# Two groups of eight mixer tiles by seven products, the other six plainly at the stage's end; the residual on VectorE straight from PSUM

## The chip, the cores and the metric

The kernel runs on one core of one Trainium2 chip. A core has five engines with a queue of instructions each: TensorE (PE in the profile, its weight loads PEld), VectorE (DVE), ScalarE (ACT), GpSimd (POOL) and SyncE (SP), which here only issues DMAs. Data lie in SBUF (128 partitions); matmuls write PSUM, eight banks of 128 x 512 floats. The metric is the device time of one execution in microseconds (us).

## The reference

A trunk of four layers on x (512 tokens, 1024 features, float32). Each layer is a token mixer (convolution, neighbourhood attention, retention, convolution) and then a gated channel mixer, each behind an RMS norm and added to x. Cut to what matters here:

```python
D_MODEL, SEQ, DEPTH = 1024, 512, 4
FFN_DIM = 2816                      # 22 tiles of 128

def conv_ffn(h, w_up, dw_w, dw_b, w_down):
    u = dwconv(h @ w_up, dw_w, dw_b)        # 5632 columns, 3 taps over tokens
    val, gate = jnp.split(u, 2, axis=-1)
    return (jax.nn.gelu(gate) * val) @ w_down

for i in range(DEPTH):
    h = rmsnorm(x, norm1_g[i])
    x = x + token_mixer(i, h)
    h = rmsnorm(x, norm2_g[i])
    x = x + conv_ffn(h, ffn_w_up[i], ffn_dw_w[i], ffn_dw_b[i], ffn_w_down[i])
```

## The kernel before

**Layout and precision.** x stays in SBUF, features on partitions, as eight tiles `x[0]` to `x[7]` of 128 x 512. A float32 product is made of three: each operand is split into a high part (cast to fp32r) and a low part (the rest), and `mm3` (L168 to L171) issues high x high, high x low, low x high. Weights come by DMA on SP into the two buffers `wr`; `split_w` (L161 to L166) casts the high part on ACT (L164) and subtracts on DVE (L165), into three buffers each of `wh` and `wl`. `prep` (L226, called `after` where a stage ends) makes the next stage's input from a tile of x: high part on ACT (L236), low part on DVE (L239), and `squares` (L250), a square on ACT whose sum into `sqacc` is made on POOL by default (L257).

**The mixer stage, `ffn` (L283).** It runs once for each layer. The 44 column tiles of the up-projection (`up`, L288, 24 wide matmuls each) are made in pairs, value and gate. `mid(j)` (L323) applies the three taps, gelu and product to pair j and gives tile j of the hidden layer, 22 in all; TensorE works on `ups_of` (L511) for the next pair meanwhile.

**Seven products.** The down-projection takes two hidden tiles (a pair of tiles, as two halves of the inner dimension), two outputs (`x[2i]`, `x[2i+1]`) and two halves of the tokens, and multiplies the 2 x 2 blocks by seven products instead of eight (Strassen-Winograd). `mid` builds the seven sums of the hidden side in F and splits them into Hh and Hl (four slots of each, `SLOT_H`); `weights` (L392) builds those of the weights: two are loaded, one is accumulated by a POOL DMA (L402), others are summed on DVE. `prod` (L420) issues one product over the pairs of a part, three narrow matmuls (256 columns) a pair. `down(q)` (L444) runs part q for the four output pairs i: products 1, 6, 0, 4, 5 in the banks xb and v, then, one output pair later, `finish` (products 2 and 3 and the add L451 into `x[2i+1]`).

**The residual of a part.** `x[2i+1]` is carried by the tile s12: ACT copies (L467, L470) and a POOL DMA that accumulates x onto it (L474); L451 then adds it to the bank v. `x[2i]` goes likewise: ACT copies the negated bank xc to u2, a POOL DMA accumulates x (L487), and DVE subtracts v (L488). In the last output pair of the last part (`direct`) DVE does it without a DMA.

**Order in a stage.** Tiles 0 and 1 (`REST`) are kept out of the products. `PARTS` groups the other ten pairs as 3, 3 and 4. The first two parts start inside the stage, after pairs 8 and 14 of the up-projections, and `filler` puts the next pair of up-projections between the last output pair's products and its `finish`. At the end of the stage stand `remainder` (tiles 0 and 1 plainly, ACT copy, POOL DMA accumulating into x) and the part of four pairs, after each of whose outputs `after` prepares the input of the next stage.

Of the kernel before, what the change touches and what calls it, by code (L numbers as in the profile page):

```python
# [70 lines left out]
PARTS = ((0, 3), (3, 6), (6, 10))  # L71
PART_COL = (0, 1536, 3072)
REST = 2
SLOT_H = 4
NT_FFN = 7
# [5 lines left out]
def tile_trunk(  # L81
# [168 lines left out]
    def squares(k, src, perm=False, eng=nc.gpsimd, wait=False):  # L250
        sq = t512() if k else sqacc
        nc.scalar.activation(sq.rearrange("p (c r) -> p r c", r=8) if perm else sq, src, AF.Square)
        if k == 0 and wait:
            state["wait"] = nc.gpsimd.tensor_copy(sm(1), xlo[KD - 1][:, :1].bitcast(F32))
        if k:
            with tc.issue_after(state["wait"].ins) if wait else ExitStack():
                eng.tensor_tensor(sqacc, sq, sqacc, ADD)  # L257
# [25 lines left out]
    def ffn(l, after):  # L283
        with ExitStack() as st:
            stage_pools(st, NT_FFN, 8, 0)
            hp = st.enter_context(tc.tile_pool(name=nm("ffn"), bufs=1, reuse_waits=RW))
            last = len(PARTS) - 1
# [35 lines left out]
            def mid(j, pv, pg):  # L323
# [17 lines left out]
                if j < REST:  # L341
                    nc.vector.tensor_tensor(acc[0], acc[0], acc[1], MUL)
                    hi = hp.tile([P, T], F32R, tag=f"rh{j}", name=nm("hh"))
                    lo = hp.tile([P, T], F32R, tag=f"rl{j}", name=nm("hl"))
                    split(acc[0], hi, lo)
                    rest[j] = (hi, lo)
                    return
                p = (j - REST) // 2
# [43 lines left out]
            def weights(i, q, gate=None):  # L392
# [14 lines left out]
                r2 = hp.tile([P, T], F32, tag="w2", name=nm("w2"))  # L407
                nc.vector.tensor_tensor(r2[:, :n], r13[:, n:2 * n], r1[:, :n], ADD)
                h2 = hp.tile([P, T], F32R, tag="h2", name=nm("h2"))
                l2 = hp.tile([P, T], F32R, tag="l2", name=nm("l2"))  # L410
                split(r2[:, :n], h2[:, :n], l2[:, :n])
                nc.vector.tensor_tensor(sg[:, :n], r2[:, :n], sg[:, n:2 * n], ADD)
# [15 lines left out]
            def rest_weights(c, gate):  # L428
                with tc.issue_after(gate.ins):
                    raw = load_raw(f_rest[l, :, c], D)  # L430
                return split_w(raw, D, nc.vector)

            def remainder(ws):
                for c, (wh, wl) in enumerate(ws):
                    for o in range(4):
                        ps = bank(psa)
                        for k in range(REST):
                            s = slice((o * REST + k) * P, (o * REST + k + 1) * P)
                            mm3(ps, wh[:, s], wl[:, s], *rest[k], k == 0, k == REST - 1)
# [4 lines left out]
            def down(q, first, pieces=iter(()), filler=None):  # L444
                final = q == last
                p0, p1 = PARTS[q]

                def finish(i, w, v, s12):
# [3 lines left out]
                    if final:  # L452
                        after(2 * i + 1)

                prev = None
                for i in range(4):
                    w = weights(i, q) if i else first
                    direct = final and i == 3
# [19 lines left out]
                    u2h, vh, xh2 = (t.rearrange("p (h t) -> p h t", h=2) for t in (u2, v, x[2 * i]))  # L478
                    if direct:
                        nc.scalar.activation(u2[:, :256], xc, AF.Copy, scale=-1.0)  # L480
                        nc.vector.tensor_tensor(x[2 * i], x[2 * i], v, SUB)
                        nc.vector.tensor_tensor(
                            xh2, xh2, u2h[:, :1, :].broadcast_to([P, 2, 256]), ADD)
                    else:
                        nc.scalar.activation(
                            u2h, xc.unsqueeze(1).broadcast_to([P, 2, 256]), AF.Copy, scale=-1.0)
                        nc.gpsimd.dma_start(u2, x[2 * i], accum_op=ADD)  # L487
                        nc.vector.tensor_tensor(x[2 * i], u2, v, SUB)  # L488
                    if final:
                        after(2 * i)  # L490
# [26 lines left out]
            starts = {REST + 2 * p1: q for q, (_, p1) in enumerate(PARTS[:-1])}  # L517
            for j in range(1, FT):
# [745 lines left out]
def _layout(inp):  # L1264
# [72 lines left out]
    for i in range(4):  # L1337
        units = [fd[:, REST + 2 * p0 + par:REST + 2 * p1:2, :, o] for p0, p1 in PARTS
# [4 lines left out]
    frest = fd[:, :REST].transpose(0, 2, 3, 1, 4).reshape(4, P, 2, 8 * P)  # L1343
# [41 lines left out]
```

## Time and profile before

| | |
|---|---|
| median of 3 runs | 2635.16 us (2627.26 to 2635.94) |
| profiled execution, its own time | 2636.45 us |
| span of the trace | 2634.7 us |
| mean granted clock of TensorE | 0.987 |
| chain that ended last, by engine | PE 81%, DMA 7%, DVE 6%, ACT 3%, issue 2% |
| DMA | 334.98 MB, mean 127 GB/s |

The busy shares of the engines stand at the head of the prediction. In the profile's rows "out<-in" names the tiles of the program without their numbers; "[8.39 <-DVE x L488]" means that the engine was idle for 8.39 us before the instruction, and that DVE's instruction of line 488 on tile x ended the wait. Groups of instructions give busy time and the mean of one in ns, then the idle time before them and its releasers. Times within the span are counted from its start.

### The profile page before, as it was taken

To read this page: it belongs to the slowest core of one execution; us is meant where nothing else is said; L and a number is where in the kernel's file an instruction comes from. 1 tells how busy PE (TensorE), PEld (TensorE's weight loads), DVE (VectorE), ACT (ScalarE), POOL (GpSimd) and SP (SyncE) were. 2 spreads that over 40 slices of the span, in tenths; PEclk is the share of its full clock that TensorE was granted. 3 is DMA by queue.
4 is the path that set the end of the run, shared out by engine and by line. 5 is a ranking of instruction groups with operands and counts; after the bars stand their busy time and mean duration, and the time that the engine had idled before them with its cause. 6 is when DMAs were issued, how large, how long until landed. Compare 5 with 4: busy or idle time off the path is not lost.

```text
span 2634.7 us, 37842 instructions
## 1 busy us (share of the span) xinstructions
PE 2548.7 (97%) x14788; PEld 2176.6 (83%) x14788; DVE 1839.4 (70%) x2934; ACT 1210.3 (46%) x1711; POOL 407.4 (15%) x469
## 2 busy tenths in 40 slices
PE   9999999979999999998999999999998999999999
PEld 7888888879998888887888888878888788788888
DVE  7977665767877776676666565776667687676675
ACT  5454444455656444454422323444445445444444
POOL 2113001034421110112000000201102221100102
PEclk9999999989999999998999999999999999999999
DMA  7724555563333355565222222245647572255656
GB/s 244 229 78 149 131 138 136 145 140 93 94 91 83 96 144 142 125 162 122 88 77 69 87 74 71 88 130 130 143 139 167 169 223 82 85 143 124 155 155 141
DMA packets 118452, 334.98 MB, mean 127 GB/s; under 512 B 14289, under 2 KB 29265, under 8 KB 118273
## 3 DMA queue, kind: packets, MB, share of 16 engines
q1 hardware_dynamic: 87216, 266.81, 33.0%
q0 software_dynamic: 29760, 63.02, 13.4%
q8 instruction: 116, 1.90, 0.3%
q10 hardware_dynamic: 1296, 2.72, 0.3%
q14 instruction: 64, 0.52, 0.1%
HBM read 291.64 MB, written 5.63 MB: 113 GB/s over the span
## 4 chain that ended last, share of the span: by engine, by line
PE 81%; DMA 7%; DVE 6%; ACT 3%; issue 2%; POOL 0%; DVEq 0%; SPq 0%; ACTq 0%; POOLq 0%
PE ps L171 22%; PE ps L169 22%; PE ps L170 22%; PE ps L175 3%; PE ps L176 3%; PE ps L174 3%; DMA t<-x 2%; DMA ws<-in_f_down 2%; DMA wr<-in_f_down 1%; DVE wl L165 1%; DMA wr<-in_f_up 1%; PE ps L648 1%; PE ps L647 1%; PE ps L646 1%; ACT wh L164 1%
## 5 line engine op out<-in xcount | busy, mean ns | idle before, releaser
L169 PE MATMUL ps<-xh,wh 128*128 128x512 f32 x1856 | 734.0, 397 | 19.2 <-ACT wh L164 19.1
L171 PE MATMUL ps<-xh,wl 128*128 128x512 f32 x1856 | 736.8, 398 | 0.1
L170 PE MATMUL ps<-xl,wh 128*128 128x512 f32 x1856 | 734.7, 396 | 0.1
L164 ACT CAST wh<-wr 128x1024 fp32r<-128x1024 f32 (+1 forms) x370 | 380.9, 1031 | 689.2 <-PE ps L170 418.9
L165 DVE TENSOR_TENSOR wl<-wr,wh 128x1024 fp32r<-128x1024 f32 (+1 forms) x367 | 445.6, 1215 | 217.0 <-ACT wh L164 197.0
L169 PEld LDWEIGHTS ps<-xh,wh 128*128 128x128 f32 x1856 | 350.1, 189 | 105.5 <-ACT wh L164 23.6
L170 PEld LDWEIGHTS ps<-xl,wh 128*128 128x128 f32 x1856 | 350.2, 189 | 85.0 <-DVE xl L239 0.5
L171 PEld LDWEIGHTS ps<-xh,wl 128*128 128x128 f32 x1856 | 350.0, 189 | 82.2 <-DVE wl L165 0.5
L169 PE MATMUL ps<-Hh,wh 128*128 128x256 f32 x640 | 178.7, 287 | 11.1 <-ACT t L470 8.2
L170 PE MATMUL ps<-Hl,wh 128*128 128x256 f32 x640 | 179.9, 286 | 4.8 <-DVE Hl L180 4.8
L171 PE MATMUL ps<-Hh,wl 128*128 128x256 f32 x640 | 175.3, 288 | 0.6 <-DVE wl L165 0.6
L169 PE MATMUL ps<-Hh,h 128*128 128x256 f32 x480 | 140.2, 292 | 30.6 <-DVE x L488 28.7
L402 POOL DMA_DIRECT2D ws<-in_f_down x48 | 42.3, 882 | 777.1 <-DMA ws<-in_f_down 744.4
L175 PE MATMUL ps<-wl,xh 128*128 128x256 f32 (+1 forms) x512 | 159.1, 312 | 1.4 <-DVE wl L165 1.4
L176 PE MATMUL ps<-wh,xl 128*128 128x256 f32 (+1 forms) x512 | 159.1, 312 | 0.6 <-DVE zz L755 0.6
L174 PE MATMUL ps<-wh,xh 128*128 128x256 f32 (+1 forms) x512 | 158.7, 313 | 0.6 <-ACT xh L236 0.6
L171 PE MATMUL ps<-Hh,l 128*128 128x256 f32 x480 | 139.2, 290 | 0.8 <-DVE l L180 0.8
L170 PE MATMUL ps<-Hl,h 128*128 128x256 f32 x480 | 139.2, 290 | 0.0
L169 PEld LDWEIGHTS ps<-Hh,wh 128*128 128x128 f32 x640 | 121.0, 191 | 15.1 <-ACT t L470 9.4
L170 PEld LDWEIGHTS ps<-Hl,wh 128*128 128x128 f32 x640 | 122.3, 191 | 7.2 <-DVE Hl L180 6.2
L169 PEld LDWEIGHTS ps<-Hh,h 128*128 128x128 f32 x480 | 95.2, 198 | 34.4 <-DVE x L488 26.5
L171 PEld LDWEIGHTS ps<-Hh,wl 128*128 128x128 f32 x640 | 119.0, 192 | 3.0 <-DVE wl L165 2.1
(301 smaller groups left out, 5078.3 us busy)
## 6 DMA issues: line engine op xcount, KB each, us to landing
wr<-in_f_up SPq DMA_DIRECT2D x176, 512.0 KB, 3.7
wraw<-in_cdw SPq DMA_DIRECT2D x56, 608.0 KB, 5.1
t<-x POOLq DMA_DIRECT2D x88, 256.0 KB, 4.0
wr<-in_cw_in SPq DMA_DIRECT2D x30, 512.0 KB, 4.4
ws<-in_f_down SPq DMA_DIRECT2D x32, 384.0 KB, 5.4
ws<-in_f_down POOLq DMA_DIRECT2D x32, 384.0 KB, 7.0
wr<-in_f_down SPq DMA_DIRECT2D x32, 384.0 KB, 4.1
wr<-in_nat_qkv SPq DMA_DIRECT2D x24, 512.0 KB, 4.1
```

The lines of the kernel that those rows point to most:

```text
L164: nc.scalar.copy(hi[:, :n], raw[:, :n])
L165: eng.tensor_tensor(lo[:, :n], raw[:, :n], hi[:, :n].bitcast(F32), SUB)
L169: nc.tensor.matmul(o, wh, ah, start=first, stop=False, skip_group_check=free)
L170: nc.tensor.matmul(o, wh, al, start=False, stop=False, skip_group_check=free)
L171: nc.tensor.matmul(o, wl, ah, start=False, stop=last, skip_group_check=free)
L174: nc.tensor.matmul(o, ah, wh, start=first, stop=False)
L175: nc.tensor.matmul(o, ah, wl, start=False, stop=False)
L176: nc.tensor.matmul(o, al, wh, start=False, stop=last)
L402: nc.gpsimd.dma_start(r13[:, :2 * n], src[:, c:c + 2 * n], accum_op=ADD)
L646: nc.tensor.matmul(o, xg[:, 0, q], W[:, 0, w], start=a == 1, stop=False)
L647: nc.tensor.matmul(o, xg[:, 0, q], W[:, 1, w], start=False, stop=False)
L648: mm = nc.tensor.matmul(o, xg[:, 1, q], W[:, 0, w], start=False, stop=a == 3)
```

## The change

- `PARTS` becomes two parts of four pairs (hidden tiles 0 to 15), which start after pairs 8 and 16 of the up-projections. Tiles 16 to 21 (`REST = 16`) are done plainly at the end of the stage by the new function `down_rest`, output by output, in `GROUPS` of three, two, two and one; in a group the last tile's matmuls come after all the others. The six tiles lie in the slots Hh and Hl that the parts have left, three to a slot. The plain weights are laid out for each output, 128 x 768.
- `x[2i]` is made by two DVE subtractions straight from the banks v and xc; the ACT copy to u2 and its POOL DMA go. The s12 path stays.
- At the end DVE adds the bank to x (`residual`), and `after` follows for each output; in the last layer the last output is added and stored in two halves.
- Inside a part all four output pairs come first, then `late` (the next `mid`), then `filler`, and then the last `finish`.
- The sum r2 of the weights is made in place in r13, and the buffer w2 goes; temporaries go from 7 to 9. In `down_rest` the squares' sum runs on DVE (`state["sq"]`).

```diff
-PARTS = ((0, 3), (3, 6), (6, 10))
-PART_COL = (0, 1536, 3072)
-REST = 2
+PARTS = ((0, 4), (4, 8))
+PART_COL = (0, 2048)
+REST = 16
+GROUPS = ((0, 1, 2), (3, 4), (5, 6), (7,))
 SLOT_H = 4
-NT_FFN = 7
+NT_FFN = 9
...
-    def squares(k, src, perm=False, eng=nc.gpsimd, wait=False):
+    def squares(k, src, perm=False, eng=None, wait=False):
+        eng = eng or state.get("sq", nc.gpsimd)
...
-                r2 = hp.tile([P, T], F32, tag="w2", name=nm("w2"))
-                nc.vector.tensor_tensor(r2[:, :n], r13[:, n:2 * n], r1[:, :n], ADD)
+                r2 = r13[:, n:2 * n]
+                nc.vector.tensor_tensor(r2, r2, r1[:, :n], ADD)
...
-            def remainder(ws):
-                for c, (wh, wl) in enumerate(ws):
-                    for o in range(4):
-                        ps = bank(psa)
...
-                        t = t512()
-                        nc.scalar.copy(t, ps)
-                        nc.gpsimd.dma_start(x[c * 4 + o], t, accum_op=ADD)
...
-                    if direct:
-                        nc.vector.tensor_tensor(s12, x[2 * i + 1], s12, ADD)
-                    else:
-                        nc.gpsimd.dma_start(s12, x[2 * i + 1], accum_op=ADD)
+                    nc.gpsimd.dma_start(s12, x[2 * i + 1], accum_op=ADD)
                     prod(v[:, :256], w["s1"], q, 4, True)
+                    nc.vector.tensor_tensor(x[2 * i], x[2 * i], v, SUB)
                     prod(xc, w["s3"], q, 5, False)
-                    u2 = t512()
...
-                        nc.scalar.activation(
-                            u2h, xc.unsqueeze(1).broadcast_to([P, 2, 256]), AF.Copy, scale=-1.0)
-                        nc.gpsimd.dma_start(u2, x[2 * i], accum_op=ADD)
-                        nc.vector.tensor_tensor(x[2 * i], u2, v, SUB)
-                    if final:
-                        after(2 * i)
+                    xh2 = x[2 * i].rearrange("p (h t) -> p h t", h=2)
+                    nc.vector.tensor_tensor(
+                        xh2, xh2, xc.unsqueeze(1).broadcast_to([P, 2, 256]), SUB)
                     if prev:
                         finish(*prev)
                     prev = (i, w, v, s12)
-                    next(pieces, None)
-                for _ in pieces:
-                    pass
-                if filler:
-                    filler()
+                late()
+                filler()
                 finish(*prev)
+
+            def down_rest():
+                kn = FT - REST
+                for group in GROUPS:
+                    open_ = {}
+                    for o in group:
+                        wh, wl = load_w(f_rest[l, o], kn * P)
+                        open_[o] = bank(psa), wh, wl
+                        for k in range(kn - 1):
+                            s = slice(k * P, (k + 1) * P)
+                            mm3(open_[o][0], wh[:, s], wl[:, s], *rest[REST + k], k == 0, False)
+                    s = slice((kn - 1) * P, kn * P)
+                    for o, (ps, wh, wl) in open_.items():
+                        mm3(ps, wh[:, s], wl[:, s], *rest[FT - 1], False, True)
+                        if l == DEPTH - 1 and o == KD - 1:
...
+                        else:
+                            residual(o, ps)
+                            after(o)
...
-            starts = {REST + 2 * p1: q for q, (_, p1) in enumerate(PARTS[:-1])}
+            starts = {2 * p1: q for q, (_, p1) in enumerate(PARTS)}
...
                 if w0:
-                    done += 1
-                    down(starts[j], w0, mid(j, ups[2 * j], ups[2 * j + 1]), lambda: ups_of(j + 1))
-            gate = state["load"]
-            ws = [rest_weights(c, gate) for c in range(2)]
-            w0 = weights(0, last, gate)
+                    down(starts[j], w0, lambda: mids(j + 1), lambda: ups_of(j + 1))
             mids(FT)
-            remainder(ws)
-            down(last, w0)
+            state["sq"] = nc.vector
+            down_rest()
+            del state["sq"]
```

The change moves instructions on several queues. On POOL, the first part of the first mixer stage reads as follows before; L402 is the accumulate of a weight tile, L474 that of s12 and L487 that of u2, and x_79 to x_86 are `x[0]` to `x[7]`.

```order
L402 DMA ws_3213<-in_f_down 128x768
L402 DMA ws_3315<-in_f_down 128x768
L402 DMA ws_3419<-in_f_down 128x768
L402 DMA ws_3522<-in_f_down 128x768
L474 DMA t_3258<-x_80 128x512
L487 DMA t_3307<-x_79 128x512
L474 DMA t_3343<-x_82 128x512
L487 DMA t_3392<-x_81 128x512
L474 DMA t_3447<-x_84 128x512
L487 DMA t_3496<-x_83 128x512
L474 DMA t_3550<-x_86 128x512
L487 DMA t_3599<-x_85 128x512
```

The same place of the changed kernel, where L406 is the accumulate of a weight tile and L455 that of s12:

```order
L406 DMA ws_3213<-in_f_down 128x1024
L406 DMA ws_3323<-in_f_down 128x1024
L406 DMA ws_3441<-in_f_down 128x1024
L406 DMA ws_3559<-in_f_down 128x1024
L455 DMA t_3257<-x_80 128x512
L455 DMA t_3350<-x_82 128x512
L455 DMA t_3468<-x_84 128x512
L455 DMA t_3586<-x_86 128x512
```

The four u2 transfers have left the queue; the four weight accumulates stand ahead of the s12 transfers as before, and are larger.

On DVE, at the end of the first mixer stage (the last outputs), before; L488 and L451 finish outputs, L482 and L472 are the direct form of the last pair, L239 is the low part for the next stage, L180 and L165 prepare weights:

```order
L488 TENSOR_TENSOR x_83<-t_5446,ps_5381 128x512
L239 SCALAR_TENSOR_TENSOR xl_99<-x_83,png,xh_91 128x8x64
L451 TENSOR_TENSOR x_84<-ps_5381,t_5382 128x512
L180 TENSOR_TENSOR l_5508<-wq_5486,h_5507 128x1024
L239 SCALAR_TENSOR_TENSOR xl_100<-x_84,png,xh_92 128x8x64
L472 TENSOR_TENSOR t_5513<-x_86,t_5513 128x512
L165 TENSOR_TENSOR wl_5857<-wr_5854,wh_5856 128x1024
L482 TENSOR_TENSOR x_85<-x_85,t_5577 128x512
L451 TENSOR_TENSOR x_86<-ps_5512,t_5513 128x512
```

The same place of the changed kernel; L283 adds a bank to x, L166 is the weights' low part, L240 the low part for the next stage, L259 the squares' sum:

```order
L283 TENSOR_TENSOR x_84<-ps_5327,x_84 128x512
L283 TENSOR_TENSOR x_85<-ps_5349,x_85 128x512
L166 TENSOR_TENSOR wl_5450<-wr_5447,wh_5449 128x1024
L166 TENSOR_TENSOR wl_5456<-wr_5453,wh_5455 128x1024
L240 SCALAR_TENSOR_TENSOR xl_100<-x_84,png,xh_92 128x8x64
L259 TENSOR_TENSOR sqacc<-t_5371,sqacc 128x512
L240 SCALAR_TENSOR_TENSOR xl_101<-x_85,png,xh_93 128x8x64
L283 TENSOR_TENSOR x_86<-ps_5389,x_86 128x512
L259 TENSOR_TENSOR sqacc<-t_5380,sqacc 128x512
L166 TENSOR_TENSOR wl_5625<-wr_5622,wh_5624 128x1024
L240 SCALAR_TENSOR_TENSOR xl_102<-x_86,png,xh_94 128x8x64
```

The adds now read a bank and x alone, no tile that a DMA has filled (t_5446, the u2 of before), and the squares' sums have come from POOL into DVE's queue.

On TensorE, at the end of the plain stage's first group in the changed kernel: ps_5174, ps_5196 and ps_5218 are the banks of outputs 0 to 2, which take the last tile's (Hh_5078) matmuls, and ps_5265 and ps_5287 those of outputs 3 and 4, which begin with tile 16 (Hh_4767):

```order
L171 MATMUL ps_5174<-Hl_5079,wh_5170 128x512
L172 MATMUL ps_5174<-Hh_5078,wl_5171 128x512
L171 MATMUL ps_5196<-Hl_5079,wh_5192 128x512
L172 MATMUL ps_5196<-Hh_5078,wl_5193 128x512
L170 MATMUL ps_5218<-Hh_5078,wh_5214 128x512
L171 MATMUL ps_5218<-Hl_5079,wh_5214 128x512
L172 MATMUL ps_5218<-Hh_5078,wl_5215 128x512
L170 MATMUL ps_5265<-Hh_4767,wh_5261 128x512
L171 MATMUL ps_5265<-Hl_4768,wh_5261 128x512
L170 MATMUL ps_5287<-Hh_4767,wh_5283 128x512
L171 MATMUL ps_5287<-Hl_4768,wh_5283 128x512
L172 MATMUL ps_5265<-Hh_4767,wl_5262 128x512
```

The scheduler has put the matmuls of outputs 3 and 4 with the high weights ahead of the first that reads a low part, wl_5262.

More of the change, by code (lines that the diff above doesn't have):

```diff
@@ L286, in ffn @@
             hp = st.enter_context(tc.tile_pool(name=nm("ffn"), bufs=1, reuse_waits=RW))
-            last = len(PARTS) - 1
             def up(n):
@@ L340, in mid @@
                 nc.scalar.activation(acc[1], acc[1], AF.Gelu_apprx_tanh)
-                if j < REST:
+                if j >= REST:
                     nc.vector.tensor_tensor(acc[0], acc[0], acc[1], MUL)
[L343 to L346, printed above, removed]
+                    r = j - REST
+                    if r % 3 == 0:
+                        for h in "hl":
+                            t = hp.tile([P, 7, 256], F32R, tag=f"H{h}{r // 3}", name=nm("H" + h))
+                            cur_f[h] = t.rearrange("p a b -> p (a b)")
+                    rest[j] = [cur_f[h][:, r % 3 * T:(r % 3 + 1) * T] for h in "hl"]
+                    split(acc[0], *rest[j])
                     return
-                p = (j - REST) // 2
+                p = j // 2
                 if j % 2 == 0:
@@ L426, in prod, with down @@
                         start and p == p0, stop and p == p1 - 1, True)
[L428 to L431, printed above, removed]
-            def remainder(ws):
-                for c, (wh, wl) in enumerate(ws):
-                    for o in range(4):
-                        ps = bank(psa)
-                        for k in range(REST):
-                            s = slice((o * REST + k) * P, (o * REST + k + 1) * P)
-                            mm3(ps, wh[:, s], wl[:, s], *rest[k], k == 0, k == REST - 1)
-                        t = t512()
-                        nc.scalar.copy(t, ps)
-                        nc.gpsimd.dma_start(x[c * 4 + o], t, accum_op=ADD)
-            def down(q, first, pieces=iter(()), filler=None):
-                final = q == last
+            def down(q, first, late, filler):
                 p0, p1 = PARTS[q]
@@ L451, in finish @@
                     nc.vector.tensor_tensor(x[2 * i + 1], v, s12, ADD)
-                    if final:
-                        after(2 * i + 1)
                 prev = None
@@ L457, in down @@
                     w = weights(i, q) if i else first
-                    direct = final and i == 3
                     xb, v = bank(psa), bank(psa)
@@ L493, in down @@
                     prev = (i, w, v, s12)
-                    next(pieces, None)
-                for _ in pieces:
-                    pass
-                if filler:
-                    filler()
-                finish(*prev)
+                late()
+                filler()
+                finish(*prev)
+            def down_rest():
[12 more added lines that the diff above has]
+                        if l == DEPTH - 1 and o == KD - 1:
+                            for c in (slice(0, 256), slice(256, 512)):
+                                nc.vector.tensor_tensor(x[o][:, c], ps[:, c], x[o][:, c], ADD)
+                                store(o, c)
+                        else:
+                            residual(o, ps)
+                            after(o)
             ups = up_first()
@@ L1337, in _layout @@
     for i in range(4):
-        units = [fd[:, REST + 2 * p0 + par:REST + 2 * p1:2, :, o] for p0, p1 in PARTS
+        units = [fd[:, 2 * p0 + par:2 * p1:2, :, o] for p0, p1 in PARTS
                  for o, par in ((2 * i + 1, 0), (2 * i, 1), (2 * i, 0), (2 * i + 1, 1))]
```

14 lines of the change are left out of this document (3 added, 11 removed).

## Prediction

> **What bounds the kernel now.** I read the busy row of the page first, then the four mixer stages in a table of stretches, then TensorE's waits.
>
> ```profile
> PE 2548.7 (97%) x14788; PEld 2176.6 (83%) x14788; DVE 1839.4 (70%) x2934; ACT 1210.3 (46%) x1711; POOL 407.4 (15%) x469
> ...
> 206.96:596.57 389.61, 369.44 (x1953) 314.75 (x1952) 263.74 (x339) 183.30 (x240) 60.22 (x73) 0.97 0.55 139
> 851.73:1240.60 388.87, 369.25 (x1953) 314.75 (x1952) 267.37 (x348) 181.50 (x247) 53.29 (x54) 0.97 0.52 131
> 1672.98:2057.43 384.45, 365.95 (x1953) 311.98 (x1952) 261.15 (x339) 178.19 (x240) 44.98 (x48) 0.98 0.52 132
> 2259.07:2634.70 375.63, 363.90 (x1952) 309.92 (x1952) 252.33 (x330) 168.07 (x226) 38.70 (x43) 0.99 0.53 135
> sum 1538.56, PE 1468.55 PEld 1251.40 DVE 1044.58 ACT 711.06 POOL 197.18; mean PE 367.14 PEld 312.85 DVE 261.14 ACT 177.77 POOL 49.30
> ```
>
> Columns: the stretch and its length, then busy us (and count) of PE, PEld, DVE, ACT, POOL, the granted clock, the DMA share and GB/s. Each row runs from the first matmul of a mixer stage to the first of the next stage (the last to the end of the span). TensorE is the bound: 1468.6 of 1538.6 us. So two things count: the matmuls' pace, and the 70.0 us in which it is idle.
>
> ```profile
> 430.17 0.28 PE L169 MATMUL ps<-Hh,h 128*128 128x256 f32 x1
> ...
> 431.96 0.28 PE L169 MATMUL ps<-Hh,h 128*128 128x256 f32 x1
> ...
> 461.51 0.40 PE L169 MATMUL ps<-xh,wh 128*128 128x512 f32 x1
> ...
> 468.05 0.39 PE L170 MATMUL ps<-xl,wh 128*128 128x512 f32 x1
> ```
>
> The first pair of starts lies 15 matmuls apart, so 0.119 us each for 256 columns; the second lies 28 apart, 0.2336 each for 512. (The rows' own durations, 0.28 and 0.40 us, overlap one another and are not the pace.) A stage now issues 1104 of the wide and 840 of the narrow kind, and 8 transposes (0.7 us): 257.9 + 100.0 + 0.7 = 358.6, over four stages 1434. Busy time is 1468.6, so another 34 us are matmuls that ran slowly, after gaps; of this below.
>
> ```profile
> PE ps L169 <- DVE x L488: 28.7, 6, 8.8
> PE ps L169 <- ACT wh L164: 20.6, 16, 2.7
> PE ps L169 <- ACT t L470: 8.7, 7, 2.4
> PE ps L170 <- DVE Hl L180: 4.8, 7, 1.2
> ```
>
> TensorE's longest waits (total, times, longest): all in the mixer. L488 is the residual add that reads what a DMA has accumulated; L164 is the cast of weights.
>
> ```profile
> 560.00:596.57 36.57, 23.11 (x156) 22.04 (x155) 23.07 (x25) 19.20 (x24) 9.49 (x7) 0.81 0.35 80
> 1204.00:1240.60 36.60, 24.71 (x169) 23.84 (x168) 21.28 (x25) 15.58 (x25) 8.11 (x7) 0.77 0.33 80
> 2021.00:2057.43 36.43, 24.52 (x180) 23.65 (x179) 22.32 (x26) 16.70 (x26) 8.12 (x7) 0.81 0.38 87
> 2600.00:2630.80 30.80, 28.38 (x218) 27.29 (x217) 15.45 (x20) 9.51 (x15) 3.50 (x5) 0.95 0.48 121
> ```
>
> The four stage ends: idle 13.5, 11.9, 11.9 and 2.4, together 39.7 us, at a clock of 0.77 to 0.81 in the first three. One of them in detail (POOL, DVE, PE):
>
> ```profile
> 1221.98 0.87 POOL L487 DMA_DIRECT2D t<-x  x1 [3.30 <-ACT t L485]
> 1227.97 0.69 DVE L488 TENSOR_TENSOR x<-t,ps 128x512 f32<-128x512 f32 x1 [4.05 <-DMA t<-x]
> 1228.71 0.58 PE L169 MATMUL ps<-Hh,h 128*128 128x256 f32 x1 [8.39 <-DVE x L488]
> 1229.09 0.41 PE L170 MATMUL ps<-Hl,h 128*128 128x256 f32 x1
> 1229.31 0.41 PE L171 MATMUL ps<-Hh,l 128*128 128x256 f32 x1
> ```
>
> The DMA issued at 1221.98 carries x into u2; DVE can add only when it is there, at 1227.97; the finishing products write the bank that this add reads, so TensorE stands for 8.39 us, and then starts matmuls 0.21 us apart instead of 0.119.
>
> The fillers, the up-projections issued inside a part, stall too, for the same DMA one step removed:
>
> ```profile
> 336.64 0.69 DVE L488 TENSOR_TENSOR x<-t,ps 128x512 f32<-128x512 f32 x1 [2.78 <-DMA t<-x]
> 338.44 0.56 DVE L408 TENSOR_TENSOR w<-ws,wr 128x384 f32<-128x384 f32 x1
> 339.02 7.27 SPq L155 DMA_DIRECT2D wr<-in_f_up  x3
> 343.64 1.04 ACT L164 CAST wh<-wr 128x1024 fp32r<-128x1024 f32 x1 [3.14 <-DMA wr<-in_f_up]
> 344.74 0.51 PE L169 MATMUL ps<-xh,wh 128*128 128x512 f32 x1 [2.36 <-ACT wh L164]
> ```
>
> DVE waits 2.78 us for the accumulate; L408 behind it frees the raw weight buffer late, the filler's load goes out at 339.02, its cast starts at 343.64, and TensorE loses 2.36 us. Eight parts of this kind (two a stage) at about 2.3 us: 18 us of the 20.6 that TensorE waits for L164.
>
> **The change, part by part.** *Matmuls.* Two pairs fewer by products: 2 x 4 x 7 x 3 = 168 narrow matmuls less, 20.0 us; four tiles more plainly: 8 x 4 x 3 = 96 wide ones more, 22.4 us. TensorE gets **2.4 us a stage, 9.7 us in all, more work**: the change pays on its own path before it gains anything.
>
> *Ends.* The last thing in a stage is now plain products with the residual added from PSUM, with no transfer in the chain; in the old last part u2 and the x<-t accumulates go. The idle 39.7 us of the ends go, and two smaller waits come. First, three outputs hold all three weight buffers until tile 21; output 3's low part then follows in a chain: cast, subtraction, and two residual adds ahead of it on DVE.
>
> ```profile
> L165 DVE TENSOR_TENSOR wl<-wr,wh 128x768 fp32r<-128x768 f32 x32 | 30.5, 952 | 16.0 <-PE ps L171 15.5 <-ACT wh L164 0.5
> L164 ACT CAST wh<-wr 128x768 fp32r<-128x768 f32 x32 | 26.8, 836 | 18.0 <-PE ps L170 18.0
> L488 DVE TENSOR_TENSOR x<-t,ps 128x512 f32<-128x512 f32 x44 | 30.2, 686 | 84.9 <-DMA t<-x 84.9
> L236 ACT ACTIVATE xh<-x,png 128x512 fp32r<-128x512 f32 x64 | 50.2, 790 | 61.8 <-DVE x L488 28.4 <-DVE x L281 12.9 <-DVE x L717 11.0
> ```
>
> From the matmul that frees the first buffer: cast 0.84, two adds (a DVE add out of PSUM is 0.686), subtraction 0.95, some 2.8 us with handovers; the order shown with the change has ten wide matmuls ahead of its first use, 2.3 us: 0.5 us a stage, 2 in all. Second, the entry: x7's add, cast (0.79) and low part (0.75 to 1.2, next rows) run 2.3 to 2.7 us after the last matmul, plus what ACT and DVE still have queued for x5 and x6; and the next stage holds seven of eight input tiles ready, 21 matmuls: 4.9 us at 512 columns, 2.5 at 256. So only the first stage's end (256-column matmuls follow) waits, about 2 us. **Ends: 39.7 becomes about 4.5.**
>
> *DVE in the plain stage* has per output one subtraction 0.95, one add 0.69, the low part of x and, newly, the square's sum:
>
> ```profile
> 13.30 0.75 DVE L239 SCALAR_TENSOR_TENSOR xl<-x,png,xh 128x512 fp32r<-128x512 f32 x1
> 14.34 0.69 DVE L257 TENSOR_TENSOR sqacc<-t,sqacc 128x512 f32<-128x512 f32 x1 [0.29 <-ACT t L252]
> ...
> 573.98 1.19 DVE L239 SCALAR_TENSOR_TENSOR xl<-x,png,xh 128x512 fp32r<-128x512 f32 x1
> ...
> 1212.15 3.27 DVE L239 SCALAR_TENSOR_TENSOR xl<-x,png,xh 128x512 fp32r<-128x512 f32 x2
> ```
>
> The low part takes 0.75 us alone and 1.6 beside POOL's squares (1212.15); with the squares on DVE I take 0.75, and 1.2 for the strided layout at the first stage's end (573.98). Sum 3.1 to 3.6 us an output against 18 x 0.2336 = 4.2 on TensorE: hidden, with little to spare; uncovered, it is the first rival.
>
> *Fillers.* The u2 transfers are gone from all parts, and DVE subtracts twice out of PSUM instead, 0.69 us more a pair of outputs, under 10 us of TensorE. The fillers now stand behind all four output pairs, so their loads have a pair's time (84 x 0.119 = 10 us) in hand. **18 us become 0** (bounds 0 and 18).
>
> *Part starts and the rest.* 70.0 less 39.7, 18 and the 3.9 us after the last matmul (2630.80 to 2634.70) leaves 8.4 us, mostly the last pair's low part (Hl, 4.8). Ahead of it now stand 18 narrow matmuls instead of 12, 0.7 us more cover, but 1024 columns of weights to prepare instead of 768. I take half, 4 (bounds 0 and 16). The in-place sum (L412) and the buffer w2 that goes cost no instruction; r13 is held a little longer, and three buffers cover it.
>
> *Slow matmuls.* The 34 us follow gaps:
>
> ```profile
> 446.22 0.69 PE L169 MATMUL ps<-xh,wh 128*128 128x512 f32 x1 [2.31 <-ACT wh L164]
> 446.71 0.63 PE L170 MATMUL ps<-xl,wh 128*128 128x512 f32 x1
> ```
>
> After 2.31 us idle the next start comes 0.49 us later, not 0.2336. Fewer and shorter gaps should take most of it; I keep a third, 11 (bounds 3 and 30). [...]
>
> **Sum**, against the profiled execution's 2636.45 us (span 2634.7; the runs' median is 2635.16): idle 70.0 to 3.9 + 4.5 + 0 + 4 = 12.4, so -57.6; slow matmuls 34 to 11, -23; more matmuls +9.7. That is -71: **2565 us**, 2.7% faster.
>
> **Rivals.** *DVE or ACT becomes the bound in the plain stage.* For it: DVE's 3.6 of 4.2 us in the first stage; the three-buffer ring. Against: 0.75 for the low part. If each stage lost 8 us there (a stall of 1.6 at each of four groups, and 1.7 of slow running): 2565 + 32 = 2597. *Fillers and part starts stay as they are*, since the raw weight buffers are still two and SP's queue still holds the down weights ahead of the fillers': 18 + 4 + some 8 slow, 2595. *The change does not shorten the waits at all*, they only move to other names: 2636 + 9.7, less a few, 2640, no change to be measured. *Slower:* POOL's queue. All four accumulates of a part now stand ahead of the first s12 transfer, and the fourth waits for a buffer freed only after the in-place sum's last reader. If s12 lands later than the finishing products by more than the 8 us that TensorE can work on without DVE (the next output pair's products), DVE's add for x1 blocks the low parts behind it. One stall of 8.4 us with 2 us of slow running in each of eight parts is 83 us: 2648.
>
> ```profile
> t<-x POOLq DMA_DIRECT2D x88, 256.0 KB, 4.0
> ...
> ws<-in_f_down SPq DMA_DIRECT2D x16, 512.0 KB, 5.8
> ```
>
> My count from the end of the last pair's up-projection: buffer free at 13 us (DVE's weights, the pair's sums and Hl), the load there at 19, s12 issued at 20 and landed at 24; x1's products end at 11.2 + 144 x 0.119 = 28. That is 4 us ahead of need.
>
> **How the numbers follow.** Forecast 0.70; DVE bound 0.13; fillers stay 0.09; no change 0.04; POOL's queue 0.04. Least: ends 2, rest 0, slow 3, so 2636.45 - 64 - 31 + 9.7 = 2551. The first two rivals lie at 2595 to 2597, so the range is 2550 to 2600. This kernel's measurement tells about 0.3% (8 us) from no change. Faster by more: 0.70 + 0.13 + 0.09 = 0.92; within: 0.04; slower: 0.04.
>
> **What would show it.** No "t<-x" releaser ahead of TensorE; stage stretches near 361 us of pace plus 4; no idle over 1 us at the fillers; at a stage's end one short wait on "wl" at output 3 and, after the first mixer, one on xh or xl; a clock of 0.99 in all four stages. Wrong would be: idle of TensorE put down to the residual adds or to wl in every group (first rival), to wh at the fillers (second), or DVE waiting on DMA at the s12 add (POOL's queue).

## The result, and the profile after

The changed kernel takes **2560.54 us** (median of 4 runs, 2557.24 to 2564.46) against 2635.55 us before (4 runs, 2627.26 to 2641.58): a ratio of **0.9718**, 95% interval 0.9686 to 0.975. The prediction was 2565, with a range of 2550 to 2600.

The busy row of the page, and the table of stretches for the four mixer stages of the changed kernel (the columns are those of before; each stretch again runs from the first matmul of the stage to the first of the next):

```profile
PE 2534.2 (99%) x14500; PEld 2156.0 (84%) x14500; DVE 1814.2 (71%) x2892; ACT 1144.5 (45%) x1567; POOL 285.2 (11%) x344
```

```profile
209.53:573.90 364.37, 361.44 (x1881) 305.86 (x1880) 260.27 (x330) 170.59 (x208) 30.50 (x43) 1.00 0.45 129
829.55:1200.10 370.55, 364.95 (x1881) 308.80 (x1880) 261.62 (x340) 165.47 (x214) 24.97 (x24) 0.99 0.41 117
1632.52:1995.62 363.10, 361.55 (x1881) 305.81 (x1880) 256.32 (x335) 162.72 (x207) 16.68 (x18) 1.00 0.42 119
2197.02:2562.40 365.38, 361.53 (x1880) 305.89 (x1880) 245.91 (x315) 151.60 (x190) 15.82 (x17) 1.00 0.42 118
sum 1463.40, PE 1449.46 PEld 1226.37 DVE 1024.12 ACT 650.38 POOL 87.97; mean PE 362.37 PEld 306.59 DVE 256.03 ACT 162.60 POOL 21.99
```

The mixer stages have gone from 1538.56 to 1463.40 us, 75.2 less. TensorE's idle time there has gone from 70.0 to 13.9 us, and its busy time from 1468.6 to 1449.5 although it has more to do. The whole span has become 72.3 us shorter (2634.7 to 2562.4): outside the mixer stages this execution took 2.9 us more, most of it in the first token mixer, which the change doesn't touch and which in another execution of the same kernel ended at 206.82 as before. Of the idle time, these waits of TensorE are left inside the mixer stages and at their exits:

```profile
PE ps L175 <- DVE x L283: 2.8, 1, 2.8
...
PE ps L170 <- DVE lgt L927: 1.5, 1, 1.5
PE ps L170 <- DVE u L539: 1.5, 1, 1.5
PE ps L172 <- DVE wl L166: 1.4, 1, 1.4
PE ps L170 <- ACT Hh L180: 1.3, 1, 1.3
PE ps L171 <- DVE Hl L181: 1.3, 1, 1.3
```

No wait on a transfer is among them. The first three are the exits of the first three stages, one each; the last three are the start of the first part in the second stage. With some 3.8 us from the last matmul's end to the end of the program they make up nearly all of the 13.9. The fillers have no row: none of them stalls.

One exit in detail (VectorE and TensorE at the end of the first stage; L240 prepares x[6], L283 is the last residual add, into x[7]):

```profile
572.02 1.15 DVE L240 SCALAR_TENSOR_TENSOR xl<-x,png,xh 128x512 fp32r<-128x512 f32 x1 [0.16 <-ACT xh L237]
...
573.08 0.68 DVE L283 TENSOR_TENSOR x<-ps,x 128x512 f32<-128x512 f32 x1
...
573.79 1.35 ACT L237 ACTIVATE xh<-x,png 128x512 fp32r<-128x512 f32 x1
573.90 0.36 PE L175 MATMUL ps<-wh,xh 128*128 128x256 f32 x1 [2.83 <-DVE x L283]
```

TensorE goes on as soon as x[7] has been added (573.76), while the cast of x[7]'s high part has only just begun (573.79). So it doesn't wait for the data of x[7]. In the built program the waiting matmul reads x[0], and the bank that it writes is the one that the last output was summed in (bank 0 for both, at all three exits).

### The profile page after: what moved, and what is told of

Same layout as the page of the kernel before. It is cut to its first block, busy times and chain, and to the rows that moved or that the text cites. A ratio compares the mean times of both kernels' runs of the same rounds, so it can differ in the third digit from the quotient of the medians.

```text
span 2562.4 us, 36584 instructions
## 1 busy us (share of the span) xinstructions
PE 2534.2 (99%) x14500; PEld 2156.0 (84%) x14500; DVE 1814.2 (71%) x2892; ACT 1144.5 (45%) x1567; POOL 285.2 (11%) x344
## 4 chain that ended last, share of the span: by engine, by line
PE 94%; DVE 3%; ACT 1%; issue 1%; DMA 0%; SPq 0%; DVEq 0%; ACTq 0%
PE ps L171 26%; PE ps L172 26%; PE ps L170 26%; PE ps L175 3%; PE ps L176 3%; PE ps L177 3%; PE ps L634 1%; PE ps L633 1%; PE ps L632 1%; PE ps L384 1%; PE ps L389 1%; PE ps L385 1%; DVE wl L166 1%; PE ps L873 0%; ACT xh L237 0%
## 5 line engine op out<-in xcount | busy, mean ns | idle before, releaser
L165 ACT CAST wh<-wr 128x1024 fp32r<-128x1024 f32 (+1 forms) x378 | 388.6, 1032 | 794.9 <-PE ps L171 510.3
L166 DVE TENSOR_TENSOR wl<-wr,wh 128x1024 fp32r<-128x1024 f32 (+1 forms) x375 | 455.4, 1215 | 309.3 <-ACT wh L165 308.2
L171 PE MATMUL ps<-Hl,wh 128*128 128x256 f32 (+1 forms) x704 | 220.3, 314 | 1.3 <-DVE Hl L181 1.3
L172 PE MATMUL ps<-Hh,wl 128*128 128x256 f32 (+1 forms) x704 | 219.5, 315 | 1.8 <-DVE wl L166 1.4
L170 PE MATMUL ps<-Hh,wh 128*128 128x256 f32 (+1 forms) x704 | 216.7, 313 | 1.3 <-ACT Hh L180 1.3
L172 PEld LDWEIGHTS ps<-Hh,wl 128*128 128x128 f32 x704 | 133.1, 190 | 12.1 <-DVE wl L166 3.7
L171 PEld LDWEIGHTS ps<-Hl,wh 128*128 128x128 f32 x704 | 133.6, 190 | 10.3 <-DVE Hl L181 1.5
L170 PEld LDWEIGHTS ps<-Hh,wh 128*128 128x128 f32 x704 | 132.0, 189 | 11.1 <-ACT Hh L180 1.5
L333 ACT ACTIVATE t<-ps,par 128x512 f32<-128x512 f32 x154 | 118.4, 775 | 1.2 <-PE ps L172 1.2
L341 ACT ACTIVATE t<-t 128x512 f32<-128x512 f32 x88 | 55.3, 630 | 141.9 <-DVE t L337 141.7
L337 DVE SCALAR_TENSOR_TENSOR t<-ps,par,t 128x511 f32<-128x511 f32 x154 | 115.0, 748 | 3.7
L335 DVE SCALAR_TENSOR_TENSOR t<-ps,par,t 128x511 f32<-128x511 f32 x154 | 114.5, 744 | 0.0
L406 POOL DMA_DIRECT2D ws<-in_f_down x32 | 28.3, 884 | 759.3 <-DMA ws<-in_f_down 251.4
```

Source lines behind the costliest of these rows:

```text
L165: nc.scalar.copy(hi[:, :n], raw[:, :n])
L166: eng.tensor_tensor(lo[:, :n], raw[:, :n], hi[:, :n].bitcast(F32), SUB)
L170: nc.tensor.matmul(o, wh, ah, start=first, stop=False, skip_group_check=free)
L171: nc.tensor.matmul(o, wh, al, start=False, stop=False, skip_group_check=free)
L172: nc.tensor.matmul(o, wl, ah, start=False, stop=last, skip_group_check=free)
L333: nc.scalar.activation(a, u, AF.Identity, bias=pc("fdb", l * 44 + c), scale=pt[:, w + 1:w + 2])
```

## The experiments

Each kernel is compared with runs of the kernel before on the same chip. The median of those was 2626.4 us beside experiments 1, 2, 5 and the first edit of 6; 2629.7 beside 4, 7 and the second edit of 6; and 2626.6 (one run) beside 3 and 8.

**1. The residual alone.** The kernel before, with only the new residual:

```diff
+                    nc.vector.tensor_tensor(x[2 * i], x[2 * i], v, SUB)
                     prod(xc, w["s3"], q, 5, False)
-                    u2 = t512()
...
-                        nc.gpsimd.dma_start(u2, x[2 * i], accum_op=ADD)
-                        nc.vector.tensor_tensor(x[2 * i], u2, v, SUB)
+                    xh2 = x[2 * i].rearrange("p (h t) -> p h t", h=2)
+                    nc.vector.tensor_tensor(
+                        xh2, xh2, xc.unsqueeze(1).broadcast_to([P, 2, 256]), SUB)
```

> The kernel before with one edit: x[2i] is made by two VectorE subtractions straight from PSUM in every output pair, with no copy to u2 and no accumulating transfer. Grouping and stage end stay as before. Theory A (the u2 transfers are what TensorE waits for, at the ends and at the fillers): the 28.7 us behind L488 and about 18 us behind L164 go, and some 20 of the 34 us of slow matmuls with them: 2569 us. Rival B (the products at the end of a stage are the trouble, and the wait moves on to the s12 transfer or the weights): of the 39.7 us idle at the ends 20 or more stay, fillers go: about 2600 us.

Measured: 2564.87 us, ratio 0.9763 (0.9737 to 0.9789). Its four mixer stages, and its ends (cut like those of before, the last up to the last matmul):

```profile
sum 1467.96, PE 1446.55 PEld 1238.14 DVE 1075.33 ACT 694.68 POOL 160.56; mean PE 361.64 PEld 309.54 DVE 268.83 ACT 173.67 POOL 40.14
```

```profile
539.00:575.58 36.58, 31.74 (x250) 31.04 (x249) 30.46 (x33) 25.01 (x29) 7.92 (x6) 0.95 0.41 106
1160.00:1196.95 36.95, 33.38 (x262) 32.57 (x261) 29.80 (x34) 20.40 (x31) 9.20 (x8) 0.95 0.45 114
1960.00:1996.39 36.39, 32.47 (x254) 31.49 (x253) 28.88 (x33) 19.75 (x30) 8.60 (x7) 0.95 0.43 108
2529.00:2560.30 31.30, 30.63 (x256) 30.27 (x254) 19.03 (x23) 9.10 (x13) 1.74 (x2) 1.00 0.46 120
```

No filler stalls, and the ends are idle for 13.0 us instead of 39.7, with the old grouping and the old products in them. In the mixer stages this one edit brings 70.6 us, against 75.2 for the whole change. Theory A holds; the rival's 20 us at the ends are not there. What TensorE still waits for at the ends is mostly ACT's copy to s12 (L467: 11.1 us in three waits).

**2. The new grouping and the plain end alone.** The changed kernel, with u2 and its transfer put back in the two parts:

```diff
-                    nc.vector.tensor_tensor(x[2 * i], x[2 * i], v, SUB)
                     prod(xc, w["s3"], q, 5, False)
...
+                    u2 = t512()
...
+                    nc.gpsimd.dma_start(u2, x[2 * i], accum_op=ADD)
+                    nc.vector.tensor_tensor(x[2 * i], u2, v, SUB)
```

> The changed kernel with x[2i] of the two parts carried by an ACT copy and an accumulating POOL transfer again, as before; plain end kept. Theory A: the fillers' stalls come back, eight of about 2.3 us, with about 8 us of slow matmuls: 2561 + 18 + 8 = 2587 us, TensorE waiting on wh by the cast. Rival (the fillers are covered by their place behind the next mid, and the transfers no longer matter): within 4 us of 2561, no such waits.

Measured: 2560.47 us, ratio 0.9749 (0.9727 to 0.9771). The sum of its mixer stages, and VectorE and the queues in the first stage's first part (L462 is u2's transfer, L463 the subtraction that waits for it, L412 the sum of weights that frees the raw buffer):

```profile
sum 1457.97, PE 1448.98 PEld 1226.16 DVE 993.14 ACT 658.24 POOL 115.69; mean PE 362.25 PEld 306.54 DVE 248.29 ACT 164.56 POOL 28.92
```

```profile
324.36 0.86 POOL L462 DMA_DIRECT2D t<-x  x1 [4.06 <-ACT t L451]
324.86 0.69 DVE L412 TENSOR_TENSOR ws<-ws,wr 128x512 f32<-128x512 f32 x1
325.63 0.33 SPq L156 DMA_DIRECT2D wr<-in_f_up  x1
326.32 1.05 ACT L165 CAST wh<-wr 128x1024 fp32r<-128x1024 f32 x1 [1.99 <-PE ps L171]
328.29 0.69 DVE L463 TENSOR_TENSOR x<-t,ps 128x512 f32<-128x512 f32 x1 [2.74 <-DMA t<-x]
```

Theory A falls here: the transfers are back, VectorE waits 2.74 us for one as it waited 2.78 before, and no filler stalls. The wait has no effect because the sum of weights now runs ahead of it (L412 at 324.86; before, L408 ran behind it, at 338.44), and the filler's load goes out at 325.63. The exits of this kernel have no wait on the residual add either: its last output lies in another bank than the next stage's first (4, 2 and 4 against 0).

**3. Larger parts in the old kernel.** To see whether it is the size of a part that hides the transfer, or the place of the fillers in the new code:

```diff
-PARTS = ((0, 3), (3, 6), (6, 10))
-PART_COL = (0, 1536, 3072)
+PARTS = ((0, 4), (4, 7), (7, 10))
+PART_COL = (0, 2048, 3584)
```

> The kernel before with one edit: the parts hold 4, 3 and 3 pairs instead of 3, 3 and 4 (starts after pairs 10 and 16); all u2 transfers and the old order of fillers stay. Theory (a part of four pairs covers the transfer: 84 x 0.119 = 10 us of products an output pair instead of 63 x 0.119 = 7.5): no stall over 0.5 us at the filler of the first part in each stage, about 2.3 us as before at that of the second, some 9 us of idle less. Rival (the place of the filler behind the next mid in the changed kernel is what hid it): stalls of about 2.3 us at all eight fillers.

Measured: 2632.14 us in one run, the kernel before beside it 2626.6. At the fillers of the first part, of four pairs, TensorE waits for no filler's weights in any stage; at those of the second, of three pairs, it waits 1.55, 1.47, 1.32 and 1.25 us. The first of these:

```profile
472.56 0.50 PE L169 MATMUL ps<-xh,wh 128*128 128x512 f32 x1 [1.55 <-ACT wh L164]
```

So the size of the part covers the transfer, and the gap that is left in the smaller part is shorter than the 2.3 us expected. The rival falls. The kernel as a whole gains nothing, because the last part now has three pairs and its ends wait longer for the transfers:

```profile
PE ps L169 <- DVE x L488: 47.4, 8, 8.8
PE ps L169 <- ACT wh L164: 9.4, 13, 1.5
```

47.4 us behind L488, against 28.7 before.

**4. The plain outputs by transfer.** The changed kernel with its plain end, but the residual of the plain outputs carried as the old remainder was:

```diff
-                            residual(o, ps)
+                            t = t512()
+                            nc.scalar.copy(t, ps)
+                            nc.gpsimd.dma_start(x[o], t, accum_op=ADD)
                             after(o)
```

> The changed kernel; the plain outputs are added to x by an ACT copy and an accumulating POOL DMA, as the old remainder was, instead of VectorE from PSUM (the last output of the last layer as it was). Theory (a transfer in the chain from the last matmul to the next stage's input costs its whole landing time at the exit): from the last matmul 0.8 + about 5 for the transfer + 0.8 + 0.75 for the split = 7.4 us until x[7] is there, of which the next stage's matmuls on the seven other tiles cover 4.9 us (2.5 after the first stage): 3 to 5 us at each exit and the slow matmuls behind it, 2570 us. The bank is free at once after the copy, so the waits on the residual add go. Rival (the transfer is covered): 2556 us.

Measured: 2636.22 us in one run, 74 more than the changed kernel in the same group: all that the change had won. It is one run, but 74 us is far beyond the spread of any kernel here. ACT's rows at the end of the first stage (L488 is the new copy, L237 the next stage's high part):

```profile
566.08 0.66 ACT L488 COPY t<-ps 128x512 f32<-128x512 f32 x1
570.35 1.21 ACT L237 ACTIVATE xh<-x,png 128x512 fp32r<-128x512 f32 x1 [3.61 <-DMA x<-t]
...
572.28 0.63 ACT L488 COPY t<-ps 128x512 f32<-128x512 f32 x1
...
591.37 0.63 ACT L488 COPY t<-ps 128x512 f32<-128x512 f32 x1
```

```profile
PE ps L170 <- ACT t L488: 52.9, 2, 30.8
PE ps L175 <- ACT t L488: 22.7, 1, 22.7
```

The expectation had the right mechanism and left out what queues behind the waiting instruction. In ACT's rows the copy of each output comes only after the high part of the output before, and that waits for that output's transfer (3.61 us at 570.35). Every output costs 6.2 us of one chain (566.08 to 572.28) instead of 4.2 us of matmuls, and at the exit the next stage's first bank is freed only by the last copy, 22 to 31 us late.

**5. Sums of squares back on GpSimd.** The two lines that set `state["sq"]` taken out.

> The changed kernel with the sums of squares of the plain stage on GpSimd instead of VectorE. The low part of x is to take 1.5 us or more where it lies beside GpSimd's sums, against 0.75 alone; VectorE's work for an output becomes 0.95 + 0.69 + 1.6 = 3.2 us, still below TensorE's 4.2. Theory (there is slack in the plain stage; only the stage exits can lose, by one slower low part, 1 us each): 2561 to 2566 us. Rival (VectorE has little to spare there, and the placement carries weight): 8 us a stage, 2590 us.

Measured: 2561.39 us, ratio 0.9757 (0.9733 to 0.9781): not to be told from experiment 2 and the first edit of experiment 6, which ran beside it (0.9749 and 0.9743). The low parts at the end of the third stage, of the changed kernel and then of this one (groups of instructions on VectorE):

```profile
L240 DVE SCALAR_TENSOR_TENSOR xl<-x,png,xh 128x512 fp32r<-128x512 f32 x7 | 5.1, 746 | 0.0
```

```profile
L240 DVE SCALAR_TENSOR_TENSOR xl<-x,png,xh 128x512 fp32r<-128x512 f32 x7 | 9.1, 1333 | 0.0
```

One low part takes 0.746 us without GpSimd's sums and 1.333 on the mean among them. The difference doesn't reach TensorE except at the exits, where the last add comes later and the waits are 3.0, 2.9 and 2.9 us instead of 2.8, 1.5 and 1.5. The theory's size holds; where the sums run hardly matters.

**6. Another bank at the exit.** First one bank was skipped ahead of the last output:

```diff
                 for group in GROUPS:
+                    if group[0] == KD - 1:
+                        bank(psa)
```

> The changed kernel with one PSUM bank skipped ahead of the last plain output, so that the next stage's first matmul needn't write the bank that the last residual add reads. Theory (the waits of 2.83, 1.48 and 1.47 us at the three stage exits are for that bank, since the matmul that waits reads x[0]): the next stage starts 1.4 us after the last plain matmul at the latest in the second and third, the first gets about 1.5 us better and then waits for x[7] itself: 3 to 5 us less in all, 2556 us. Rival (it is data, or the bank is another): no change, the same three waits.

Measured: 2559.37 us, ratio 0.9743 (0.972 to 0.9766), and the same three waits, 2.7, 1.5 and 1.5 us. It decided nothing: in the built program the last output still lies in bank 0, as does the next stage's first. The next edit moves the other side, by reserving the second PSUM pool of a token mixer ahead of the first:

```diff
-        cur["a"] = st.enter_context(tc.tile_pool(name=nm("psa"), bufs=na, space=PSUM, reuse_waits=RW))
-        cur["b"] = cur["a"] if nb == 0 else st.enter_context(
-            tc.tile_pool(name=nm("psb"), bufs=nb, space=PSUM, reuse_waits=RW))
+        if nb:
+            cur["b"] = st.enter_context(tc.tile_pool(name=nm("psb"), bufs=nb, space=PSUM, reuse_waits=RW))
+        cur["a"] = st.enter_context(tc.tile_pool(name=nm("psa"), bufs=na, space=PSUM, reuse_waits=RW))
+        if nb == 0:
+            cur["b"] = cur["a"]
```

> The changed kernel; in a token mixer's stage the second PSUM pool is now reserved ahead of the first, so that the first matmul after a mixer stage writes another bank than the one of the last plain output (skipping a bank in the mixer stage left both in bank 0). Theory (the exit waits are for that bank): the waits on the residual add go at all three exits, 5.8 us of idle; the first stage's next matmuls then wait up to 1.3 us for x[7]: 4 to 6 us less than the changed kernel beside it, 2555 us. Rival (x[7]'s own data, or the slower banks of another stage, take the gap's place): within 2 us of the changed kernel.

> The changed kernel itself, beside the other kernels of this group on the same chip: about 2560 us, ratio about 0.972 to the kernel before, and the same three waits at the stage exits (2.8, 1.5, 1.5 us).

Measured, side by side: 2556.09 us (2555.91 to 2557.31), ratio 0.9724 (0.9711 to 0.9738), against 2562.03 us for the changed kernel (2557.18 to 2562.07), ratio 0.9741 (0.9728 to 0.9755). The first and the third mixer stage of the new kernel:

```profile
207.48:568.88 361.40, 361.32 (x1882) 306.02 (x1881) 257.43 (x326) 167.62 (x205) 30.42 (x43) 1.00 0.44 127
...
1626.03:1987.42 361.39, 361.30 (x1881) 306.02 (x1880) 254.65 (x327) 162.69 (x206) 16.61 (x18) 1.00 0.41 118
```

The three exit waits on the residual add are gone; in the built program the next stages' first matmuls now write banks 5, 4 and 4, and the last outputs still lie in bank 0. These two stages are 361.4 us long, which is the matmuls' pace (361.0, worked out below) and nothing more. The wait was for the bank. The four mixer stages together are 7.7 us shorter than in the profiled run of the changed kernel beside it (1455.79 against 1463.47 us). The stage after the first mixer stage gives 1.6 of that back: there TensorE waits 1.01 us for the high part of x[7], as the theory said, and 1.18 us for weights. This is the fastest kernel of the study, though the intervals of the two ratios still overlap a little.

**7. Three parts of three pairs.** `PARTS = ((0, 3), (3, 6), (6, 9))`, `REST = 18`: one pair more by products, four tiles plainly.

> Three parts of three pairs (tiles 0 to 17 by seven products, started after pairs 6, 12 and 18), and four tiles plainly: 84 narrow matmuls more (10.0 us) and 48 wide ones fewer (11.2 us) a stage, 4.9 us less in four stages. TensorE's share of a plain output falls to 12 x 0.2336 = 2.8 us, VectorE's is 0.65 + 0.69 + 0.75 + 0.69 = 2.8, and about 3.3 in the first stage with its strided layout. Theory (VectorE binds the plain stage once it has no slack, and there is a third part start): 4 us lost in the first stage, 1 to 2 in each other, so 2559 to 2567 us, no gain. Rival (VectorE's backlog is taken up by the next stage's first matmuls): 2556 us.

Measured: 2564.86 us, ratio 0.9756 (0.9742 to 0.9769), 2.8 us more than the changed kernel beside it. No gain, as the theory said, but mostly at another place: its second stage loses some 7 us at the starts of its parts (waits of 2.02, 1.32, 2.80 and 0.84 us on Hh and Hl), the plain end of the first stage only 2.2 us, and those of the other stages nothing before their exits, where the second and third stage wait 2.0 and 2.4 us instead of 1.5 each.

**8. Stalls of chosen length.** Six stalls put into the up-projections of the changed kernel's last two stages:

```diff
+                if (l, n) in STALL:
+                    t = t512()
+                    nc.vector.tensor_copy(t, ups[n - 1])
+                    for _ in range(STALL[l, n]):
+                        nc.vector.tensor_copy(t, t)
...
                 for k in range(KD):
```

> The changed kernel with six stalls of different length put into the up-projections of the last two mixer stages, far from each other: the weights of one tile wait for a chain on VectorE that starts when the tile before is done (one copy out of PSUM, then 0, 1, 2, 3, 4 or 6 copies of 128x512, two short writes), so gaps of about 1.1, 1.8, 2.4, 3.0, 3.7 and 5 us. The output is unchanged. Theory of the prediction (matmuls run at half rate after gaps of 2.3 us): half rate for some us after the gaps from about 2 us on. [...]

Measured: 2614.27 us in one run, with the stalls in it. The gaps came out longer than planned: 3.35, 4.96, 4.26, 8.25, 7.40 and 7.82 us. After each of the first four the first matmul took 0.77 us; where the rate stayed full behind a gap, at 1809.58 below, it took 0.51. The shortest (TensorE's rows):

```profile
1692.97 0.77 PE L171 MATMUL ps<-xh,wh 128*128 128x512 f32 x1 [3.35 <-DVE wh L302]
1693.54 0.63 PE L172 MATMUL ps<-xl,wh 128*128 128x512 f32 x1
1693.97 0.63 PE L173 MATMUL ps<-xh,wl 128*128 128x512 f32 x1
...
1696.10 0.44 PE L172 MATMUL ps<-xl,wh 128*128 128x512 f32 x1
1696.38 0.40 PE L173 MATMUL ps<-xh,wl 128*128 128x512 f32 x1
1696.62 0.39 PE L171 MATMUL ps<-xh,wh 128*128 128x512 f32 x1
```

Starts 0.43 us apart for 3.1 us, then 0.23 again. Half rate after gaps from about 2 us on, the theory, isn't put to the test by it, since the shortest gap came out at 3.35 us; the kernel before has shorter ones. One of its fillers:

```profile
1809.58 0.51 PE L169 MATMUL ps<-xh,wh 128*128 128x512 f32 x1 [2.31 <-ACT wh L164]
1809.92 0.39 PE L170 MATMUL ps<-xl,wh 128*128 128x512 f32 x1
```

Here the rate is full after 2.31 us, while after the 2.31 us at 446.22, which the prediction quotes, it is half. Of the eight fillers (gaps of 2.01 to 2.68 us) four were followed by half rate, for 3.41 us each. So the theory doesn't hold as it stands: gaps of this length were followed by half rate in four cases and by the full rate in four (slow matmuls, below).

## Why the prediction came out right

**Matmuls, +9.7 us: right.** A stage now has 1200 wide and 672 narrow matmuls and 8 transposes: 280.3 + 80.0 + 0.7 = 361.0 us of pace, 2.4 more than before. The stages without other waits are 361.4 us long (experiment 6).

**Ends, 39.7 to 4.5: right in size, half right in mechanism.** That the old idle time goes with the transfers was right; that 4.5 us of small waits came so near was luck, since they are other waits than those forecast. The exits of three stages wait 2.8 + 1.5 + 1.5 = 5.8 us. The first small wait of the prediction, 0.5 us a stage for the weights of output 3, isn't in the trace: no gap there is over 0.1 us. The second was put down to x[7]'s data and to the first exit alone; it is the bank, at all three exits (experiments 2 and 6). That the transfers had to leave the chain of the last outputs is shown from both sides: taking those of u2 out of the old end brings 26.7 of its 39.7 us (experiment 1), and putting them into the new end costs 74 us (experiment 4).

**Fillers, 18 to 0: right, one of the reasons misput.** The step gave two: the u2 transfers go, and an output pair's time (84 x 0.119 = 10 us) is in hand because the fillers "now stand behind all four output pairs". They did so before, too; what is new is that a part has four pairs, so that an output pair takes 10 us instead of 7.5. The runs show that each reason is enough by itself: without the u2 transfers no filler stalls in parts of three pairs (experiment 1), and in parts of four pairs none stalls although the transfers are there (experiments 2 and 3).

**Part starts, 8.4 to 4: right.** 4.0 us, all in the second stage:

```profile
935.42 0.39 PE L172 MATMUL ps<-Hh,wl 128*128 128x256 f32 x1 [1.39 <-DVE wl L166]
938.66 0.74 PE L170 MATMUL ps<-Hh,wh 128*128 128x256 f32 x4 [1.32 <-ACT Hh L180]
940.72 0.58 PE L171 MATMUL ps<-Hl,wh 128*128 128x256 f32 x1 [1.32 <-DVE Hl L181]
```

Why only this stage has them was not tried.

**Slow matmuls, 34 to 11: too cautious.** The busy time of 1449.5 us less the pace of 4 x 361.0 = 1444.0 leaves 5.5. The size was off, though within the bounds, and the reading of the slow matmuls was half right. A gap of 2.31 us brought half rate at 446.22 and none at 1809.58, and only four of the eight fillers' gaps brought it: here the length of a gap alone didn't decide. In the trace of the kernel before, half rate starts after those four at 446.36, 989.08, 1091.48 and 1910.68. These times lie 159, 30 and 240 times 3.413 us apart, and in each of the two traces, before and after, all changes between full and half clock lie on one grid of 3.413 us, to within 0.01 us. So count TensorE's busy time in each step of that grid (columns: the step and its length, busy us and count of PE, the granted clock, the DMA share and GB/s):

```profile
442.95:446.36 3.41, 1.10 (x7) 1.00 0.66 207
446.36:449.78 3.42, 3.42 (x9) 0.50 0.52 135
...
1804.87:1808.28 3.41, 2.40 (x18) 1.00 0.47 160
1808.28:1811.70 3.42, 2.12 (x9) 1.00 0.40 153
1811.70:1815.11 3.41, 3.41 (x19) 1.00 0.91 190
```

The gap before 446.22 falls into one step, and TensorE is busy for 1.10 us of it; the next step ran at half rate. The equal gap before 1809.58 is split between two steps, 2.40 and 2.12 us busy, and the clock stayed full. The other six agree: 0.73, 1.40 and 1.32 us busy in the step ahead of half rate, 1.80 or more in each where the clock stayed full. The three gaps of 1.3 to 1.4 us at the part start above fit as well: TensorE is busy for 1.42 us of the step from 936.67 to 940.09, and half rate followed for two steps. In the two traces half rate followed 16 steps of full clock, 13 of them with 0.00 to 1.49 us busy, the others with 1.54, 1.77 and 2.21; the steps that were followed by another at full clock had 1.80 us or more. What makes the clock change is not shown.

**The rivals.** That VectorE or ACT binds the plain stage falls with the trace, in which TensorE has no gap over 0.1 us inside the plain ends, with experiment 5, in which a slower low part cost nothing but the exits, and with experiment 7, whose plain outputs are a third shorter and still lose only 2.2 us in the worst stage. Fillers that stay, and waits that only move, are not in the trace. POOL's queue, the slower case, would have shown as VectorE waiting for the transfer of s12; in the trace neither VectorE nor TensorE has such a wait.

**Sum.** In the mixer stages -75.2 measured; with the 2.9 us that this execution lost elsewhere -72.3, against -71 forecast. Of the terms, the slow matmuls gave 5.5 us more than forecast, the idle time 1.5 less (70.0 to 13.9 instead of 12.4). What the prediction could not say is how the gain divides, and it doesn't add up: the residual alone brings 70.6 us in the mixer stages, grouping and plain end alone 80.6 (5.4 more than both, since its exits happen to have no bank in common), both together 75.2. Each part of the change takes the same waits away.

## What to carry to other kernels

Where two edits of one change aim at the same wait, try each alone: here either would have done, and the simpler one (two VectorE subtractions out of PSUM) keeps the old grouping. A transfer in the chain from the last matmul to the next stage's input can cost more than its own time: in experiment 4 the copies of the later outputs stood behind the instruction that waited for it, and an output cost 6.2 us instead of 4.2. At a stage's exit look at which bank the first matmul writes as well as at what it reads: here the bank cost 5.8 us at three exits. And don't price a gap by its length alone: of two of 2.31 us in the kernel before, the one that left TensorE busy for 1.10 us of a step of 3.41 us was followed by half rate, and the one that left 2.40 and 2.12 us of two steps was not.

## What was not expected

The bank that a tile gets isn't the next in a ring in the order of the program: skipping one bank, in experiment 6, changed nothing, and small edits elsewhere (experiment 2) moved the last output from bank 0 to 4 or 2, and the 5.4 us by which its mixer stages are shorter than the changed kernel's go with that. And the first token mixer, with a gap of 1.93 us in both traces (up to 133.42 before, 133.08 after), ran there at full clock before and partly at half after:

```profile
135.00:140.00 5.00, 5.00 (x65) 0.70 0.68 156
```

Before, the same stretch had 87 matmuls at a clock of 1.00. The grid of the clock lies differently in the two executions: here TensorE is busy for 1.48 us of the step from 131.13 to 134.54, and half rate followed; before, the step from 132.34 to 135.75 has 2.33 us, and the clock stayed full. Of the four runs of the changed kernel two had a mean clock of 0.996 (2564.46 and 2563.47 us) and two of 0.999 (2557.24 and 2557.61 us): the 6 us that separate the runs go with it.
